# Feed-forward: the 16-bit halves of h transposed by the DMA engines, between two copies

## The chip, the core and the metric

The kernel runs on one core of a Trainium2 chip. Five engines work side by side, each in the order of its own instructions: TensorE (PE in the profile; PEld is its weight load), VectorE (DVE), ScalarE (ACT), GpSimd (POOL) and SyncE (SP), which here only issues DMAs. They wait for each other by semaphores. The metric is device time in microseconds, the median of several runs.

## The reference

A trunk of two layers over x of 256 tokens by 1024, all float32. Each layer is a half-step feed-forward, a mixer (a gated linear recurrence beside a forgetting attention), and a second half-step feed-forward:

```
def swiglu_ffn(h, w_up, w_down):
    gate, up = jnp.split(h @ w_up, 2, axis=-1)
    return (jax.nn.silu(gate) * up) @ w_down

for l in range(2):
    x = x + 0.5 * swiglu_ffn(rms_norm(x, g_ffn1[l]), w_up1[l], w_down1[l])
    h = rms_norm(x, g_mix[l])
    ...                                   # the mixer, x = x + m @ w_o[l]
    x = x + 0.5 * swiglu_ffn(rms_norm(x, g_ffn2[l]), w_up2[l], w_down2[l])
```

The feed-forward is 2816 wide, so `w_up` is 1024 x 5632 and `w_down` 2816 x 1024. The change is in the four feed-forwards alone.

## The kernel before

**Products in three passes.** Each float32 operand is split in a rounded high part and the rest, and a product is made of three matmuls (L364 to L366: high x high, low x high, high x low). Tokens are worked in two tiles of 128. A matmul takes a 128x128 block of transposed activations as the stationary operand and 512 weight columns (256 in the last chunk) as the moving one.

**Weights.** They come in pieces of 512 KB, each two or four row blocks of 128. SyncE loads a piece into one of five `raw` buffers (L300), ScalarE casts it to the high part `whi` (L324), VectorE subtracts that to get the low part `wlo` (L333); `whi` and `wlo` have six buffers each. A load is issued when the subtraction has freed a `raw` buffer. A piece of 512 columns serves 12 matmuls, 6 per token tile.

**A feed-forward** goes over six chunks of the 2816 columns, five of 512 and one of 256. For a chunk TensorE makes the gate block, both token tiles, then the up block. ScalarE takes the gate out of PSUM with silu (L589), VectorE multiplies with the up product into a tile `nat` (L594): this is h of the chunk, with tokens on partitions. The down product needs h with columns on partitions. `h_chain` does that: TensorE transposes blocks of 128x128 against an identity into a PSUM bank `z` (L448), ScalarE writes the rounded high part from there (L469), VectorE the rest (L471), into the tile `hT` (`s` in the profile). The down product of chunk c is made behind the up block of chunk c+1; those of chunks 4 and 5 are made together at the end, in the order token tile 0, column half 0 and 1, then token tile 1, and chunk 5 right behind chunk 4 in each. The output of each is added to x (L538), and in the feed-forwards that have a successor x is transposed and scaled for the next stage (L448, L481, L469, L471).

**The order** of each engine's instructions is made when the program is built, by a list scheduler (`Sched`) that keeps a clock for TensorE, ScalarE and VectorE with a cost for each operation. Side work such as `h_chain` is written as a generator, which yields the time at which its next step may go and the engine; between matmuls `hook` runs the steps that are due. `copy_any` gives a copy to ScalarE or VectorE, whichever would end first by the clock. Buffers are claimed from rings: three `tmp`, four `nat`, four `z` banks.

Of the kernel before, what the change touches and what calls it, by code (L numbers as in the profile page):

```python
# [7 lines left out]

F32 = mybir.dt.float32
F32R = mybir.dt.float32r  # L10
AF = mybir.ActivationFunctionType
ALU = mybir.AluOpType
AX = mybir.AxisListType

P = 128
# [136 lines left out]
def act_c(n, ap=0):  # L152
    return 0.11 + 0.000833 * n + 0.093 * ap


def dve_c(n):
    return 0.09 + 0.00104 * n
# [3 lines left out]
def hybrid_encoder_kernel(  # L161
# [6 lines left out]
    nc = tc.nc  # L168
    S = Sched()
# [20 lines left out]
    def new(pool, shape, tag, dt=F32):  # L190
        return pool.tile(shape, dt, tag=tag, name=nm(tag))
# [3 lines left out]
    def new_nat(n=512):  # L195
        r = S.claim(nat_ring, NNAT)
        return new(nat_p, [P, n], "nat"), r

    def new_tmp(shape=None):
        r = S.claim(tmp_ring, NTMP)  # L200
        return new(tmp_p, shape or [P, 512], "tmp"), r

    def bank(pool, tag):
        return pool.tile([P, 512], F32, tag=tag, name=nm(tag))
# [5 lines left out]
    def zbank():  # L210
        r = S.claim(z_ring, 4)
        return bank(ps_z, "z"), r
# [3 lines left out]
    def slot(shape, dt=F32):  # L216
        i = free_slots.pop(0)
        t = slot_p.tile(shape, dt, tag=f"s{i}", name=nm(f"s{i}"))
        return [t, i]
# [5 lines left out]
    def f32(ap):  # L225
        return ap.bitcast(F32)
# [20 lines left out]
    CH = [(c * 512, min(512, FF - c * 512)) for c in range(6)]  # L247
# [55 lines left out]
    def copy_any(out_, in_, n, dep, fast=False):  # L303

        a = max(S.t["a"], dep, S.now) + act_c(n)
        d = max(S.t["d"], dep, S.now) + dve_c(n if not fast else n // 2)
        if d < a:
            nc.vector.tensor_copy(out_, in_)
            S.t["d"] = d
        else:  # L310
            nc.scalar.copy(out_, in_)
            S.t["a"] = a
        return min(a, d) + LAT
# [5 lines left out]
    def emit_hi():  # L319
        i = nxt["hi"]  # L320
        nxt["hi"] += 1
        _, nk, ncol = hcs[i]
        hi = new(whi_p, [P, nk, ncol], "whi", F32R)
        nc.scalar.copy(hi, raws[i])  # L324
        his[i] = hi, S.use("a", act_c(1024))

    def emit_lo():
# [3 lines left out]
        hi, end = his.pop(i)  # L331
        lo = new(wlo_p, [P, nk, ncol], "wlo", F32R)
        nc.vector.tensor_tensor(out=lo, in0=raws.pop(i), in1=f32(hi), op=ALU.subtract)  # L333
# [23 lines left out]
    def visit(i, acc, lhs, k0, tok, first, last, fin=None):  # L357

        hi, lo = get_hc(i)
        _, nk, ncol = hcs[i]  # L360
        ts = slice(tok * P, tok * P + P)
        for kk in range(nk):
            st, sp = first and kk == 0, last and kk == nk - 1
            nc.tensor.matmul(acc, lhsT=lhs(0, k0 + kk)[:, ts], rhs=hi[:, kk, :], start=st, stop=False)  # L364
            nc.tensor.matmul(acc, lhsT=lhs(0, k0 + kk)[:, ts], rhs=lo[:, kk, :], start=False, stop=False)  # L365
            nc.tensor.matmul(acc, lhsT=lhs(1, k0 + kk)[:, ts], rhs=hi[:, kk, :], start=False, stop=sp)  # L366
            S.use("p", 3 * (ncol / 2400.0 + 0.0027))
            if kk == nk - 1:
                used[i] += 1
                if used[i] == NT:  # L370
                    ready.pop(i)
                if fin is not None:
                    fin()
            if kk * ncol % 512 == 0:
                S.hook()
# [3 lines left out]
    def take(n):  # L379
        i = hpos[0]  # L380
        hpos[0] += n
        return i
# [63 lines left out]
    def quad(src, dst_ps, n=4):  # L446
        for j in range(n):
            nc.tensor.transpose(dst_ps[:, j * P:(j + 1) * P], src[:, j * P:(j + 1) * P], ident)  # L448
        S.use("p", 0.112 * n)

    def k4(ps, n=4):
        return ps.rearrange("p (k t) -> p k t", k=4)[:, :n, :]

    def scale_any(out_, in_, scale, n, fast=False):
# [6 lines left out]
        else:  # L461
            nc.scalar.activation(out_, in_, AF.Copy, scale=scale)
            S.t["a"] = a
        return min(a, d) + LAT

    def split_seg(t, hi, lo, n=512):

        yield S.now, "a"
        nc.scalar.copy(hi, t)  # L469
        yield S.use("a", act_c(n)), "d"  # L470
        nc.vector.tensor_tensor(out=lo, in0=t, in1=f32(hi), op=ALU.subtract)  # L471
        S.use("d", dve_c(n))
# [15 lines left out]
    def sum_chain(tok, hf, dep):  # L488
        yield dep, "a"
        junk, rj = new_tmp()  # L490
        nc.scalar.activation(junk, xn[:, tok, hf * 512:(hf + 1) * 512], AF.Square,
                             accum_out=ssq[:, tok, hf:hf + 1])
# [10 lines left out]
    def new_xT():  # L503
        return [slot([P, KD, T], F32R), slot([P, KD, T], F32R)]

# [30 lines left out]
    def x_update(tok, hf, acc, alpha, nxn):  # L536
        xs = xn[:, tok, hf * 512:(hf + 1) * 512]
        nc.vector.scalar_tensor_tensor(out=xs, in0=acc, scalar=alpha, in1=xs, op0=ALU.mult, op1=ALU.add)  # L538
        dep = S.use("d", dve_c(512))
        if nxn is None:  # L540
            nc.sync.dma_start(out=out[0, tok * P:(tok + 1) * P, hf * 512:(hf + 1) * 512], in_=xs)
        else:
            nxn.start(tok, hf, dep)

    def rs(tok):
        return rstd[:, tok:tok + 1]
# [6 lines left out]
    def ffn(nrm, nxn, mixed=0):  # L553
        lhs = nrm.lhs()
        hT = {}
        hch = {}
        dacc = {}

        def h_chain(c, tok, h, rh, dep):
            yield dep, "p"  # L560
            m = CH[c][1] // P
            ps, rz = zbank()
            quad(h, ps, m)
            rh.free = True
            ts = slice(tok * P, (tok + 1) * P)
            yield from split_seg(k4(ps, m), hT[c][0][:, 0, :m, ts], hT[c][0][:, 1, :m, ts], m * P)
            rz.free = True

        def down(c, tok, hf, i0, last):
            m = CH[c][1] // 256  # L570
            if (tok, hf) not in dacc:
                dacc[tok, hf] = bank(ps_x, "x") if tok == 0 else bank(ps_y, "y")
            S.need(hch[c, tok])
            src = lambda e, k, h=hT[c][0]: h[:, e, k, :]
            for i in range(m):
                fin = None
                if last and i == m - 1:
                    fin = lambda: x_update(tok, hf, dacc[tok, hf], 0.5, nxn)
                visit(i0 + i, dacc[tok, hf], src, 2 * i, tok, c == 0 and i == 0, last and i == m - 1, fin)

        for c, (f0, n) in enumerate(CH):
            hT[c] = slot([P, 2, 4, T], F32R)
            s = {}

            def ev_g(tok, acc):
                nrm.scaled(tok)
                s[tok] = new_nat(n)
                S.func("silu")
                nc.scalar.activation(s[tok][0], acc, AF.Silu, scale=rs(tok))  # L589
                S.use("a", act_c(n, 1))  # L590

            def ev_u(tok, acc):
                h, rh = s[tok]
                nc.vector.scalar_tensor_tensor(out=h, in0=acc, scalar=rs(tok), in1=h, op0=ALU.mult, op1=ALU.mult)  # L594
                dep = S.use("d", dve_c(n), S.t["a"])
                hch[c, tok] = rh.user = S.add(h_chain(c, tok, h, rh, dep), dep)

            block(lhs, ev_g, xbank if c < mixed else zbank, n, nrm if c == 0 else None, c < mixed)
            block(lhs, ev_u, zbank, n)
            if 0 < c < 5:  # L600
                for hf in range(2):
                    i0 = take(2)
                    for tok in range(NT):
                        down(c - 1, tok, hf, i0, False)
                free(hT[c - 1])
        nrm.release()
        i0 = take(6)
        for tok in range(NT):
            for hf in range(2):
                down(4, tok, hf, i0 + 3 * hf, False)  # L610
                down(5, tok, hf, i0 + 3 * hf + 2, True)
        free(hT[4])
        free(hT[5])
# [4 lines left out]
    def load_fw(l):  # L618
        r, rr = new_tmp([P, KD, H])
        nc.sync.dma_start(out=r, in_=w_in[l, :, OFF_F:OFF_F + H].rearrange("(k p) n -> p k n", p=P))  # L620
        w = const.tile([P, KD, 2 * H], F32R, tag="fw", name=nm("fw"))
        fw[l] = w
# [7 lines left out]
    def logsig(dst, src, n):  # L630
# [8 lines left out]
        S.func("exp")  # L639
        nc.scalar.activation(e, e, AF.Exp)  # L640
        yield S.use("a", 0.22), "d"
# [12 lines left out]
    def mix(l, nrm):  # L654
# [12 lines left out]
        def conv_chain(hf, nats, dep):  # L667
            yield dep, "p"
            for jj in range(2):
# [10 lines left out]
                for j in range(2):  # L680
                    n = hf * 4 + 2 * jj + j
                    z, y = ps[:, j, :], xr[0][:, n, :]
                    yield S.now, "a"
                    nc.scalar.activation(y, z, AF.Identity, scale=col(R_CW + 3 * 8 + n), bias=col(R_CB + n))
                    yield S.use("a", act_c(T, 2)), "d"
# [55 lines left out]
        def cum_chain(lfs):  # L741
# [7 lines left out]
            yield S.use("p", 0.75), "a"  # L749
            nc.scalar.activation(cum, ps[:, :T], AF.Copy, scale=sgn)  # L750
            S.use("a", act_c(T, 1))
            rz.free = True

        def lru_chain():
# [76 lines left out]
            free(th)  # L831
            ghT[0], ghT[1] = slot([P, KD, T], F32R), slot([P, KD, T], F32R)
            for hf in range(2):
# [391 lines left out]
```

## Time and profile before

| | |
|---|---|
| median of 3 runs | 1305.29 us (1305.26 to 1306.33) |
| the profiled execution | 1305.66 us, its span 1303.9 us |
| TensorE busy | 1287.2 us, 99% |
| VectorE, ScalarE busy | 815.5 us (63%), 706.5 us (54%) |
| DMA, load queue of SyncE | 228.75 MB, 55.6% of 16 engines |
| granted TensorE clock | 1.00 |

Busy shares are means over the whole span; a stretch of one stage tells what an engine's work costs there. Matmuls are pipelined and overlap in the profile, so the cost of one is the distance of two starts, not its duration.

### The profile page before, as it was taken

The numbers are of one execution on the slowest core, as the hardware profiler recorded it, in microseconds if no ns is written. First come the engines' busy times: TensorE is split into PE (matmuls) and PEld (weight loads), VectorE is DVE, ScalarE is ACT, GpSimd is POOL, SyncE is SP. The second block draws the span as 40 slices with busy tenths as digits, with TensorE's granted clock in tenths as the row PEclk, the third lists the DMA queues.
The fourth block names the chain that finished last, engine by engine and source line by source line (L and its number), as shares of the span: only waits on it lengthen the run. The fifth ranks groups of instructions, "written<-read, shape, count | busy, mean of one in ns | idle before, by whom it ended". The sixth has DMA issues, their size and how long they took to land.

```text
span 1303.9 us, 16570 instructions
## 1 busy us (share of the span) xinstructions
PE 1287.2 (99%) x6209; PEld 1065.9 (82%) x6209; DVE 815.5 (63%) x1131; ACT 706.5 (54%) x988; POOL 84.8 (7%) x85
## 2 busy tenths in 40 slices
PE   8999999999999999999999999999999999999998
PEld 6888888887778888888888888888877788888887
DVE  5655558799765666555575555678987567655553
ACT  6544446776865455444454444558768554544442
POOL 5000001005100000000000000000250000000000
PEclk9999999999999999999999999999999999999999
DMA  8655557365446565555565565574654455555551
GB/s 273 198 188 184 181 161 217 123 191 154 118 142 201 181 194 194 184 182 183 162 208 183 192 194 182 156 212 126 181 146 145 145 195 172 189 190 192 192 186 59
DMA packets 128896, 229.92 MB, mean 176 GB/s; under 512 B 9848, under 2 KB 22320, under 8 KB 128816
## 3 DMA queue, kind: packets, MB, share of 16 engines
q1 hardware_dynamic: 127968, 228.75, 55.6%
q8 instruction: 49, 0.80, 0.2%
q0 software_dynamic: 832, 0.11, 0.1%
q14 instruction: 31, 0.25, 0.1%
q10 hardware_dynamic: 16, 0.00, 0.0%
HBM read 227.78 MB, written 1.05 MB: 175 GB/s over the span
## 4 chain that ended last, share of the span: by engine, by line
PE 91%; DVE 6%; ACT 1%; issue 1%; DMA 1%; SPq 0%; DVEq 0%; ACTq 0%
PE x L364 13%; PE x L365 13%; PE x L366 13%; PE z L364 12%; PE z L366 12%; PE z L365 12%; PE z L448 4%; PE y L364 3%; PE y L366 3%; PE y L365 3%; DVE wlo L333 2%; PE z L934 1%; PE z L762 1%; PE y L992 1%; DVE s L824 1%
## 5 line engine op out<-in xcount | busy, mean ns | idle before, releaser
L333 DVE TENSOR_TENSOR wlo<-raw,whi 128x1024 fp32r<-128x1024 f32 x424 | 515.9, 1226 | 251.2 <-ACT whi L324 243.2
L324 ACT CAST whi<-raw 128x1024 fp32r<-128x1024 f32 x424 | 442.4, 1050 | 319.9 <-PE z L366 136.8
L364 PE MATMUL x<-whi,s 128*128 128x512 f32 x832 | 337.3, 405 | 1.5 <-ACT whi L324 1.3
L365 PE MATMUL x<-wlo,s 128*128 128x512 f32 x832 | 325.3, 391 | 1.9 <-DVE wlo L333 1.1
L366 PE MATMUL x<-whi,s 128*128 128x512 f32 x832 | 325.3, 391 | 0.1
L364 PE MATMUL z<-whi,s 128*128 128x512 f32 (+1 forms) x752 | 282.5, 376 | 0.0
L366 PE MATMUL z<-whi,s 128*128 128x512 f32 (+1 forms) x752 | 279.7, 372 | 0.0
L365 PE MATMUL z<-wlo,s 128*128 128x512 f32 (+1 forms) x752 | 279.6, 372 | 0.0
L366 PEld LDWEIGHTS x<-whi,s 128*128 128x128 f32 x832 | 156.3, 188 | 34.1 <-DVE s L471 0.5
L364 PEld LDWEIGHTS x<-whi,s 128*128 128x128 f32 x832 | 156.5, 188 | 33.7 <-issue 2.1
L365 PEld LDWEIGHTS x<-wlo,s 128*128 128x128 f32 x832 | 156.7, 188 | 32.4 <-DVE wlo L333 2.0
L366 PEld LDWEIGHTS z<-whi,s 128*128 128x128 f32 x752 | 141.8, 189 | 24.9
L365 PEld LDWEIGHTS z<-wlo,s 128*128 128x128 f32 x752 | 141.9, 189 | 23.7
L364 PEld LDWEIGHTS z<-whi,s 128*128 128x128 f32 x752 | 141.8, 189 | 23.7
L589 ACT ACTIVATE nat<-z,rstd 128x512 f32<-128x512 f32 (+1 forms) x46 | 30.0, 653 | 77.7 <-PE z L366 77.6
L364 PE MATMUL y<-whi,s 128*128 128x512 f32 x176 | 71.0, 403 | 0.0
L366 PE MATMUL y<-whi,s 128*128 128x512 f32 x176 | 68.9, 391 | 0.0
L365 PE MATMUL y<-wlo,s 128*128 128x512 f32 x176 | 68.7, 391 | 0.0
L594 DVE SCALAR_TENSOR_TENSOR nat<-z,rstd,nat 128x512 f32<-128x512 f32 (+1 forms) x48 | 33.8, 704 | 54.2 <-PE z L366 54.2
L469 ACT CAST s<-z 128x512 fp32r<-128x512 f32 (+1 forms) x56 | 31.1, 555 | 66.9 <-PE z L448 66.5
L501 POOL TENSOR_TENSOR rstd<-msum,mhalf 128x1 f32<-128x1 f32 x12 | 11.8, 985 | 819.4 <-ACT whi L324 524.5
L471 DVE TENSOR_TENSOR s<-z,s 128x512 fp32r<-128x512 f32 (+1 forms) x56 | 36.4, 650 | 29.7 <-ACT s L469 29.7
(152 smaller groups left out, 933.7 us busy)
## 6 DMA issues: line engine op xcount, KB each, us to landing
raw<-in_w_up_dram SPq DMA_DIRECT2D x176, 512.0 KB, 4.6
raw<-in_w_in_dram SPq DMA_DIRECT2D x112, 512.0 KB, 4.3
raw<-in_w_down_dram SPq DMA_DIRECT2D x88, 512.0 KB, 4.4
raw<-in_w_lru_out_dram SPq DMA_DIRECT2D x16, 512.0 KB, 4.7
raw<-in_w_attn_out_dram SPq DMA_DIRECT2D x16, 512.0 KB, 4.7
raw<-in_w_o_dram SPq DMA_DIRECT2D x16, 512.0 KB, 5.3
tmp<-in_b_gate_dram SPq DMA_DIRECT2D x8, 256.0 KB, 4.9
xn<-in_x_dram SPq DMA_DIRECT2D x4, 256.0 KB, 4.6
```

Source lines behind the costliest of these rows:

```text
L324: nc.scalar.copy(hi, raws[i])
L333: nc.vector.tensor_tensor(out=lo, in0=raws.pop(i), in1=f32(hi), op=ALU.subtract)
L364: nc.tensor.matmul(acc, lhsT=lhs(0, k0 + kk)[:, ts], rhs=hi[:, kk, :], start=st, stop=False)
L365: nc.tensor.matmul(acc, lhsT=lhs(0, k0 + kk)[:, ts], rhs=lo[:, kk, :], start=False, stop=False)
L366: nc.tensor.matmul(acc, lhsT=lhs(1, k0 + kk)[:, ts], rhs=hi[:, kk, :], start=False, stop=sp)
L448: nc.tensor.transpose(dst_ps[:, j * P:(j + 1) * P], src[:, j * P:(j + 1) * P], ident)
L469: nc.scalar.copy(hi, t)
L471: nc.vector.tensor_tensor(out=lo, in0=t, in1=f32(hi), op=ALU.subtract)
L589: nc.scalar.activation(s[tok][0], acc, AF.Silu, scale=rs(tok))
L594: nc.vector.scalar_tensor_tensor(out=h, in0=acc, scalar=rs(tok), in1=h, op0=ALU.mult, op1=ALU.mult)
L762: nc.tensor.matmul(ps[:, g, :], lhsT=wax[0][:, g, n, :], rhs=xr[0][:, n, :], start=True, stop=True)
L824: nc.vector.tensor_tensor_scan(t_[:, n, :], r[:, n, :], i_[:, n, :], 0.0, ALU.mult, ALU.add)
```

## The change

`h_chain` no longer uses TensorE, nor a PSUM bank. It claims a tile `tmp`, and a first copy splits each float32 of h into its two 16-bit halves, all the lower ones ahead of all the upper ones, the bits unchanged. A DMA from SyncE's queue transposes these 128 rows of 1024 half words (512 in the last chunk) in 16-bit blocks, back into the tile of h. A second copy puts the halves together again in `tmp`, and from there the high part and the rest are written as before, now read from SBUF. The scheduler counts 6.0 us from the end of the first copy until the second may go. Lines from L560 on stand 9 further down in the new kernel (L594 is L603), those ahead one (L311 is L312).

```
         def h_chain(c, tok, h, rh, dep):
-            yield dep, "p"
-            m = CH[c][1] // P
-            ps, rz = zbank()
-            quad(h, ps, m)
+            yield dep, "a"
+            n = CH[c][1]
+            m = n // P
+            hd, rd = new_tmp([P, n])
+            end = copy_any(hd.bitcast(U16).rearrange("p (e n) -> p e n", e=2),
+                           h.bitcast(U16).rearrange("p (n e) -> p e n", e=2), 2 * n, dep)
+            hx16 = h.bitcast(U16).rearrange("p (m t) -> p m t", t=P)
+            nc.sync.dma_start_transpose(out=hx16, in_=hd.bitcast(U16))
+            yield end + 6.0, "a"
+            end = copy_any(hd.bitcast(U16).rearrange("p (m t e) -> p e m t", e=2, t=P),
+                           hx16.rearrange("p (e m) t -> p e m t", e=2), 2 * n, S.now)
             rh.free = True
             ts = slice(tok * P, (tok + 1) * P)
-            yield from split_seg(k4(ps, m), hT[c][0][:, 0, :m, ts], hT[c][0][:, 1, :m, ts], m * P)
-            rz.free = True
+            yield end, "a"
+            yield from split_seg(hd.rearrange("p (m t) -> p m t", t=P), hT[c][0][:, 0, :m, ts], hT[c][0][:, 1, :m, ts], m * P)
+            rd.free = True
```

TensorE's order loses 48 groups of transposes of `nat` and is otherwise that of before, but for two small transposes at the start that stand some matmuls later.

The end of the second feed-forward (637 us in the trace), on ScalarE, before: the silu of the second token tile, the weight casts, the casts of h (`s_1001`) from the PSUM bank, then the next stage's.

```order
L589 ACTIVATE nat_5276<-z_5249,rstd 128x256
L324 CAST whi_5282<-raw_5179 128x1024
L469 CAST s_1001_5217<-z_5324 128x2x128
L324 CAST whi_5335<-raw_5189 128x1024
L324 CAST whi_5350<-raw_5215 128x1024
L469 CAST s_1001_5217<-z_5359 128x2x128
L469 CAST s_1024_5381<-tmp_5394 128x4x128
```

The same place now; `nat_5229` and `nat_5258` are h of the first and the second token tile, `s_999` is `hT`, a COPY of 128x512 is a first copy, one of 128x2x256 a second.

```order
L598 ACTIVATE nat_5258<-z_5231,rstd 128x256
L325 CAST whi_5264<-raw_5163 128x1024
L312 COPY tmp_5306<-nat_5229 128x512
L325 CAST whi_5315<-raw_5171 128x1024
L325 CAST whi_5330<-raw_5207 128x1024
L312 COPY tmp_5339<-nat_5258 128x512
L312 COPY tmp_5306<-nat_5229 128x2x256
L470 CAST s_999_5194<-tmp_5306 128x2x128
L470 CAST s_1024_5362<-tmp_5375 128x4x128
L492 ACTIVATE tmp_5384,ssq<-xn 128x512
L312 COPY tmp_5339<-nat_5258 128x2x256
```

The first tile's cast moved from between the weight casts to behind both of them and two copies; the second tile's second copy stands behind the next stage's first cast.

Inside a chunk (the one at 543 us), on ScalarE now; `nat_4512` and `nat_4553` are h of the two tiles, and the first copy of `nat_4512` stands on VectorE.

```order
L325 CAST whi_4634<-raw_4559 128x1024
L312 COPY tmp_4650<-nat_4553 128x1024
L312 COPY tmp_4600<-nat_4512 128x2x512
L325 CAST whi_4666<-raw_4573 128x1024
L470 CAST s_864_4477<-tmp_4600 128x4x128
L325 CAST whi_4675<-raw_4611 128x1024
L312 COPY tmp_4650<-nat_4553 128x2x512
L325 CAST whi_4705<-raw_4625 128x1024
L470 CAST s_864_4477<-tmp_4650 128x4x128
```

Before, two casts of `s` from `z` stood among these weight casts; now there are three copies and two casts.

SyncE's queue at the end of the second feed-forward, now:

```order
L301 DMA raw_5268<-in_w_up_dram 128x2x512
L301 DMA raw_5284<-in_w_up_dram 128x2x512
L568 DMA_TRANSPOSE nat_5229<-tmp_5306 128x4x128
L301 DMA raw_5334<-in_w_up_dram 128x2x512
L568 DMA_TRANSPOSE nat_5258<-tmp_5339 128x4x128
L301 DMA raw_5347<-in_w_up_dram 128x2x512
```

Before, the loads stood there alone.

## Rows read from the trace of the kernel before

**Rows 1.** Page, busy us, share of the span, instructions:
```profile
PE 1287.2 (99%) x6209; PEld 1065.9 (82%) x6209; DVE 815.5 (63%) x1131; ACT 706.5 (54%) x988; POOL 84.8 (7%) x85
```
**Rows 2.** Page, chain that ended last, by engine:
```profile
PE 91%; DVE 6%; ACT 1%; issue 1%; DMA 1%; SPq 0%; DVEq 0%; ACTq 0%
```
**Rows 3.** Stage table: stretch, length, busy us by engine, clock, DMA share, GB/s:
```profile
430.00:650.00 220.00, 220.00 (x1056) 183.91 (x1055) 124.15 (x130) 102.44 (x121) 1.43 (x2) 1.00 0.57 182
```
**Rows 4.** Groups of instructions on TensorE, 430 to 650 us, by shape:
```profile
L448 PE MATMUL z<-ident,nat 128*128 128x128 f32 x44 | 6.7, 272 | 0.0
```
**Rows 5.** In order of time, TensorE, a group of four: start us, us, engine, line:
```profile
550.63 0.39 PE L366 MATMUL x<-whi,s 128*128 128x512 f32 x1
...
551.31 0.39 PE L366 MATMUL x<-whi,s 128*128 128x512 f32 x1
551.54 0.60 PE L448 MATMUL z<-ident,nat 128*128 128x128 f32 x4
...
552.68 0.40 PE L364 MATMUL y<-whi,s 128*128 128x512 f32 x1
```
**Rows 6.** In order of time, TensorE, a group of two and the due matmul:
```profile
637.04 0.29 PE L366 MATMUL z<-whi,s 128*128 128x256 f32 x1
637.16 0.38 PE L448 MATMUL z<-ident,nat 128*128 128x128 f32 x2
...
637.62 0.28 PE L366 MATMUL z<-whi,s 128*128 128x256 f32 x1
...
642.18 0.39 PE L364 MATMUL x<-whi,s 128*128 128x512 f32 x1
```
**Rows 7.** Groups on ScalarE by shape: count, busy us, mean ns, idle before, releasers:
```profile
L324 ACT CAST whi<-raw 128x1024 fp32r<-128x1024 f32 x424 | 442.4, 1050 | 319.9 <-PE z L366 136.8 <-PE x L366 77.4 <-PE y L366 74.9
...
L469 ACT CAST s<-tmp 128x512 fp32r<-128x512 f32 x24 | 14.8, 618 | 29.2 <-DVE tmp L481 29.0
```
**Rows 8.** In order of time, VectorE, the end of the second feed-forward:
```profile
636.28 0.48 DVE L594 SCALAR_TENSOR_TENSOR nat<-z,rstd,nat 128x256 f32<-128x256 f32 x1 [0.21 <-PE z L366]
637.99 0.42 DVE L471 TENSOR_TENSOR s<-z,s 128x256 fp32r<-128x256 f32 x1 [1.22 <-ACT s L469]
...
639.78 2.35 DVE L333 TENSOR_TENSOR wlo<-raw,whi 128x1024 fp32r<-128x1024 f32 x2
```
**Rows 9.** DMA issues: count, KB each, median us from issue to landing:
```profile
raw<-in_w_up_dram SPq DMA_DIRECT2D x176, 512.0 KB, 4.6
...
s<-in_w_x_dram SPq DMA_DIRECT2D x2, 512.0 KB, 8.9
out_dram<-xn SPq DMA_DIRECT2D x4, 256.0 KB, 2.0
```
**Rows 10.** In order of time, VectorE, a chunk's two products:
```profile
543.08 0.75 DVE L594 SCALAR_TENSOR_TENSOR nat<-z,rstd,nat 128x512 f32<-128x512 f32 x1 [2.55 <-PE z L366]
...
549.88 0.74 DVE L594 SCALAR_TENSOR_TENSOR nat<-z,rstd,nat 128x512 f32<-128x512 f32 x1
```
**Rows 11.** In order of time, ScalarE, the weight casts behind them:
```profile
554.95 1.05 ACT L324 CAST whi<-raw 128x1024 fp32r<-128x1024 f32 x1 [0.33 <-PE y L366]
559.03 1.05 ACT L324 CAST whi<-raw 128x1024 fp32r<-128x1024 f32 x1 [3.02 <-PE y L366]
```
**Rows 12.** Who waited for whom: us in total, times, longest us:
```profile
ACT whi L324 <- DMA raw<-in_w_up_dram: 5.0, 4, 2.0
```
**Rows 13.** In order of time, ScalarE, the end of the second feed-forward:
```profile
637.58 0.37 ACT L469 CAST s<-z 128x256 fp32r<-128x256 f32 x1 [2.77 <-PE z L448]
...
639.38 1.06 ACT L324 CAST whi<-raw 128x1024 fp32r<-128x1024 f32 x1 [0.39 <-PE z L366]
```
**Rows 14.** In order of time, SyncE's queue:
```profile
636.10 0.37 SPq L300 DMA_DIRECT2D raw<-in_w_up_dram  x1
```

More of the change, by code (lines that the diff above doesn't have):

```diff
@@ L10 @@
 F32R = mybir.dt.float32r
+U16 = mybir.dt.uint16
 AF = mybir.ActivationFunctionType
```

## The prediction

> **What bounds the kernel now.** I read the shares of busy time first, then the chain of waits, then a stage table, then single stretches in order of time. TensorE is busy for 99% of the span, VectorE for 63% and ScalarE for 54% [rows 1], and 91% of the chain that ended last runs through TensorE [rows 2]. In the second feed-forward, from 430 to 650 us, TensorE has no gap at all at full granted clock, while VectorE works 124 and ScalarE 102 of 220 us, and the DMA engines 0.57 of the time [rows 3]. So in these stretches what is taken from TensorE is gained, and what is given to VectorE, ScalarE or DMA is free until TensorE has to wait for it.
>
> **What goes.** Each feed-forward has six chunks and two token tiles, twelve chains; four feed-forwards make 48. Forty transpose 4 blocks, eight (the last chunk, 256 columns) 2 blocks, 176 transposes. Their price is not the 272 ns that each one shows [rows 4], since matmuls overlap; it is the shift of the starts. Around a group of four, matmuls start every 0.227 us (550.63 to 551.31 is three steps); from the last one before the group at 551.31 to the fourth behind it at 552.68 are 1.37 us where four steps take 0.91 [rows 5]. That is 0.46 us for a group of four. For a group of two, 637.04 to 637.62 is 0.58 us where three steps of 0.12 take 0.36: 0.22 us [rows 6]. 40 x 0.46 + 8 x 0.22 = 20.2 us. TensorE's order is otherwise that of before, so all of it comes off, unless a wait is put in its place.
>
> **What comes: work on ScalarE and VectorE.** Two copies per chain, 96 in all, each of 1024 half words (512 in the last chunk). By the order 76 stand on ScalarE and 20 on VectorE. No 16-bit copy is in the trace. The nearest rows are the cast of 1024 elements, 1.05 us on ScalarE, and a 512-element cast from SBUF, 0.62 us [rows 7]; VectorE's subtraction of 1024 takes 1.23 us, half of the 2.35 us pair at 639.78 [rows 8]. I take these; a copy could cost half or, with the stride of two, double. 60 x 1.05 + 16 x 0.62 + 20 x 1.23 = 98 us, while ScalarE has 597 and VectorE 488 us without work [rows 1]. As load this costs nothing.
>
> **What comes: transposes on the DMA queue.** 48 transposes move 40 x 256 KB + 8 x 128 KB = 11.5 MB. At the loads' 512 KB in 4.6 us [rows 9] even one after another they are 101 us of DMA time, against 0.43 of the span free. The unknown is T, the time from issue to landing. Nothing like it is in the trace: the lower bound is 2.0 us (256 KB stored from SBUF on a queue that is empty), the upper 8.9 us (the slowest group of loads), with 4.6 us for the common load [rows 9].
>
> **Inside a chunk T is covered.** Take the chunk at 543 us. The first token's product is done at 543.83 [rows 10]; its first copy stands on VectorE and ends by 545.1. Its second copy stands on ScalarE behind the other token's first copy (the third piece of order shows both), which cannot start before 550.62 [rows 10] and ends at 551.7. So T up to 6.6 us makes nobody wait. The second token's transpose is issued at 551.7; its second copy stands behind two weight casts that before ended at 556.0, and the cast behind it started at 559.03 after 3.02 us idle [rows 11]. T up to 559.03 - 1.05 - 551.7 = 6.3 us delays no cast. The result is due only when the next chunk's gate and up are through, more than 20 us later. Longer T eats into the lead of the weights. Most of the time that ScalarE is idle before a weight cast ends with TensorE giving a buffer back [rows 7]: the six buffers are full. Five pieces, some half used, then stand ready, each of 12 matmuls, 2.7 us; I estimate the lead at two such pieces, 5 us, and a delay of less is hidden too. On the queue the first transpose stands ahead of a load; loads land in 4.6 us and ScalarE waited for one four times, 5.0 us in all [rows 12], so a load two or three microseconds late stays hidden.
>
> **At the end of a feed-forward T is not covered.** There the last chunk's first token is due at once. By the trace at 637: its product ends at 636.76 [rows 8], the first copy on ScalarE, idle until then [rows 13], at 637.4; transpose T; second copy 0.62, cast 0.37 [rows 13], subtraction 0.42 [rows 8], with the hand-overs 1.5 us. TensorE wants it at 642.18 [rows 6], less the 0.46 us of two groups removed: 641.72. The stall is 637.4 + T + 1.5 - 641.72 = T - 2.8 us. It has a floor: the second copy stands behind the weight cast that ends at 640.44 - 0.22 and the other token's first copy, so it ends at 641.5, the cast at 641.8, the subtraction at 642.3: 0.6 us even for a short T; VectorE's pair of subtractions, ending at 642.13 - 0.22 [rows 8], gives the same. For T: a load was issued on the same queue at 636.10 [rows 14] and lands 4.6 us later at 640.7; a quarter of its bytes behind it makes about 641.7, T = 4.3, my estimate, close to the common load's row. Stall 1.5 us in three ends; in the last feed-forward no load is in flight, so the floor, 0.6. Sum 5.1 us (2.4 if all are at the floor, 24.4 at T = 8.9). The second token is due some 10 us later and its chain, though behind the next stage's first cast, has about 1 us in hand: nothing.
>
> The Trainium skill speaks against the change: "VectorE: DVE Perf Modes", section The three transpose paths, lists 390 ns for a 128x128 16-bit transpose by TensorE and 1309 ns by the DMA crossbar, and its rules advise TensorE where a PSUM destination will do. If the blocks went one by one at that price, the last chunk's four would take 5.2 us, and by the formula the stall would be 2.4 us at each of four ends, and the sum 1295 instead of 1290.5. The trace here agrees on TensorE's side (272 ns shown, 115 ns of it not hidden); no run here shows the DMA's.
>
> **Sum.** The profiled execution took 1305.66 us (span 1303.9), 0.37 above the median of the runs. 1305.66 - 20.2 + 5.1 = 1290.6; by the median 1290.2. I forecast 1290.5.
>
> **Rivals.**
> A, the forecast: T of 2 to 5 us. 1288 to 1294. Chance 0.62.
> B, slow transposes, T of 5 to 8 us, still hidden inside the chunks: at T = 6.5 a stall of 3.7 us at each end, 14.8 us, 1300.3. For it: the transposes share one queue with 512 KB loads, whose landing is 4.6 us at the best of times. Against: they carry a half or a quarter of the bytes. Chance 0.18.
> C, slower: T of 9 us or more at the ends. The stall passes 20.2 / 4 = 5.05 us from T = 7.85 us on. At the row of 8.9 us it is 6.1 us, 24.4 us in all: 1309.9. In the chunks ScalarE would then stand 2 to 3 us before each second copy, which the lead still hides. For it: no row shows how the engines do a 16-bit transpose. Against: the 8.9 us row is one of 512 KB loads queued behind others. Chance 0.13.
> D, the weights come late: the queue is served in order, so each transpose holds the loads behind it until its copy is done and it is issued. If that came to 0.42 us of TensorE per chain (20.2 / 48), nothing is left: 1305. Against: the wait on loads named above is 5.0 us in the whole span, and in the order the transposes stand where the next load is not due yet. Chance 0.07, half of it within 0.2%.
> That TensorE isn't relieved can be excluded: its order lacks just these 48 groups.
>
> **Chances and range.** 0.2%, 2.6 us, is about what a measurement of this kernel tells from no change. Faster: A, B and a little of D, 0.81. Same: 0.05. Slower: C and the rest of D, 0.14. The range takes in A without any stall (1305.3 - 20.2 = 1285) and B up to T = 7: 1285 to 1302; beyond it lie C and most of D.
>
> **What would show it.** The 176 transposes gone from TensorE, and matmul starts at 0.227 us through the places where they stood. Transposes landing 2 to 5 us after issue. ScalarE's second copies not idle-waiting inside chunks by more than a microsecond. Four gaps of TensorE of 0.5 to 2 us, each before the last chunk's down matmuls, released by VectorE's subtraction. It is wrong if gaps of TensorE on weights appear inside chunks, if the four gaps are over 5 us, or if the transposes land later than 7.85 us.

## The result: 1288.1 us, 1.3% faster

The changed kernel took 1288.1 us (median of 4 runs, 1286.94 to 1288.31), the kernel before, in the same comparison, 1305.28 us; the ratio is 0.9866 (95% interval 0.9855 to 0.9878). The profiled execution took 1288.31 us, its span was 1286.6 us, and the granted clock was 0.999 of the full 2.4 GHz. In the experiments below two executions, 7418 us of the kernel before and 4533 us in experiment 6, took several times as long as the others of their kernels; medians and ratios leave them out.

From the page of the kernel after: busy time by engine, the load queue, the chain that ended last, and the groups of TensorE's first pass and of the new copies on ScalarE (count, busy us, mean ns of one, idle time before and what ended it).

```profile
PE 1266.1 (98%) x6033; PEld 1047.3 (81%) x6033; DVE 824.5 (64%) x1151; ACT 780.6 (61%) x1064; POOL 84.9 (7%) x85
...
q1 hardware_dynamic: 174560, 240.29, 62.5%
...
PE 90%; DVE 6%; ACT 2%; DMA 2%; issue 1%; SPq 0%; ACTq 0%; DVEq 0%
...
L365 PE MATMUL x<-whi,s 128*128 128x512 f32 x832 | 337.2, 405 | 5.3 <-ACT s L470 3.5
...
L312 ACT COPY tmp<-nat 128x1024 uint16<-128x1024 uint16 (+1 forms) x76 | 84.1, 1133 | 68.6 <-DMA nat<-tmp 60.7
```

Against [rows 1] TensorE has 176 instructions and 21.1 us less, ScalarE 74 us and VectorE 9 us more (consecutive instructions overlap, so busy time rises by less than the sum of what is added). The chain still runs through TensorE [rows 2]; DMA rose from 1% to 2% of it. The queue carries 11.5 MB more. New are two waits: ScalarE waited 60.7 us for transposes, and TensorE 3.5 us for ScalarE's cast of h.

The stretch of the second feed-forward, as in [rows 3]: stretch, length, busy us of PE, PEld, DVE, ACT, POOL, granted clock, DMA share, GB/s.

```profile
430.00:650.00 220.00, 218.82 (x1029) 182.61 (x1028) 129.99 (x142) 124.61 (x146) 2.82 (x3) 1.00 0.67 198
```

TensorE, without a gap there before, is idle for 1.18 us of it: one gap, at the end of the feed-forward. In order of time, after, on TensorE:

```profile
632.22 0.39 PE L367 MATMUL x<-whi,s 128*128 128x512 f32 x1
633.79 0.50 PE L365 MATMUL x<-whi,s 128*128 128x512 f32 x1 [1.18 <-ACT s L470]
634.12 0.40 PE L366 MATMUL x<-wlo,s 128*128 128x512 f32 x1
```

and on ScalarE and SyncE's queue, in the same stretch:

```profile
627.54 0.62 ACT L312 COPY tmp<-nat 128x512 uint16<-128x512 uint16 x1 [1.99 <-DVE nat L603]
628.46 1.05 ACT L325 CAST whi<-raw 128x1024 fp32r<-128x1024 f32 x1 [0.30 <-PE z L367]
629.90 1.05 ACT L325 CAST whi<-raw 128x1024 fp32r<-128x1024 f32 x1 [0.39 <-PE z L367]
630.86 0.61 ACT L312 COPY tmp<-nat 128x512 uint16<-128x512 uint16 x1
632.54 0.76 ACT L312 COPY tmp<-nat 128x512 uint16<-128x512 uint16 x1 [1.07 <-DMA nat<-tmp]
633.33 0.40 ACT L470 CAST s<-tmp 128x256 fp32r<-128x256 f32 x1
```

```profile
628.19 1.20 SPq L568 DMA_TRANSPOSE nat<-tmp  x1
631.55 0.38 SPq L301 DMA_DIRECT2D raw<-in_w_up_dram  x1
```

The first copy ends at 628.16, the transpose is issued at 628.19 and lands 4.3 us later, at 632.5. The second copy takes 0.76, the cast 0.40, and TensorE starts at 633.79. The low part isn't waited for: the first two matmuls need only the high part.

Where the group of [rows 5] stood, the last matmul ahead of it and the first behind it now start 0.23 us apart, after:

```profile
544.52 0.39 PE L367 MATMUL x<-whi,s 128*128 128x512 f32 x1
544.75 0.39 PE L365 MATMUL y<-whi,s 128*128 128x512 f32 x1
```

Every matmul of the three passes (5280) has its counterpart in the trace of before, so the shift of each start can be followed. It grows by 0.36 us at the first matmul behind each removed group of four, 0.09 at the next, and 0.05 in all over the following ten: 0.495 us, 19.8 for the 40. A group of two gives 0.21 to 0.26 us, the eight 1.9. All groups together give 21.7 us. The shift falls back for good at four places only, the ends of the feed-forwards: by 1.24, 1.34, 1.38 and 0.19 us at the matmul behind the gap, and by another 0.1 at the next one, 4.6 in all. 1305.66 - 21.7 + 4.6 = 1288.6, against 1288.31 measured; 0.2 us of the rest lies in the first 30 us, ahead of all groups. The expectations below were written with first figures of 21.4 and 4.15.

### The profile page after: what moved, and what is told of

Read it like the earlier page. It is cut to its first block, busy times and chain, and to the rows that moved or that the text cites. A ratio compares the mean times of both kernels' runs of the same rounds, so it can differ in the third digit from the quotient of the medians.

```text
span 1286.6 us, 16397 instructions
## 1 busy us (share of the span) xinstructions
PE 1266.1 (98%) x6033; PEld 1047.3 (81%) x6033; DVE 824.5 (64%) x1151; ACT 780.6 (61%) x1064; POOL 84.9 (7%) x85
## 3 DMA queue, kind: packets, MB, share of 16 engines
q1 hardware_dynamic: 174560, 240.29, 62.5%
HBM read 227.78 MB, written 1.05 MB: 178 GB/s over the span
## 4 chain that ended last, share of the span: by engine, by line
PE 90%; DVE 6%; ACT 2%; DMA 2%; issue 1%; SPq 0%; ACTq 0%; DVEq 0%
PE x L365 13%; PE x L366 13%; PE x L367 13%; PE z L366 12%; PE z L367 12%; PE z L365 12%; PE y L367 3%; PE y L365 3%; PE y L366 3%; PE z L449 2%; DVE wlo L334 2%; PE z L943 2%; PE z L771 1%; DMA nat<-tmp 1%; PE y L1001 1%
## 5 line engine op out<-in xcount | busy, mean ns | idle before, releaser
L325 ACT CAST whi<-raw 128x1024 fp32r<-128x1024 f32 x424 | 442.1, 1050 | 248.3 <-PE z L367 126.0
L312 ACT COPY tmp<-nat 128x1024 uint16<-128x1024 uint16 (+1 forms) x76 | 84.1, 1133 | 68.6 <-DMA nat<-tmp 60.7
L603 DVE SCALAR_TENSOR_TENSOR nat<-z,rstd,nat 128x512 f32<-128x512 f32 (+1 forms) x48 | 33.9, 706 | 61.0 <-PE z L367 61.0
L472 DVE TENSOR_TENSOR s<-tmp,s 128x512 fp32r<-128x512 f32 (+1 forms) x72 | 47.2, 656 | 22.6 <-ACT s L470 22.6
```

## Experiments

Each kernel ran on the same chip as runs of the kernel before, and its ratio is against these. Their median was 1305.43 us beside experiments 1 to 4 and 1304.98 beside 5 to 7 (1305.28 beside the changed kernel), so times from different chips compare to about half a microsecond.

**1. The gain alone.** h is cast as it stands, untransposed, so this kernel leaves out a step and does not compute the reference.

```
-            hd, rd = new_tmp([P, n])
...                                  # both copies and the transpose
-            yield from split_seg(hd.rearrange("p (m t) -> p m t", t=P), ...)
+            yield from split_seg(h.rearrange("p (m t) -> p m t", t=P), ...)
```

Expected: 

> Nothing transposes h: its high and low parts are taken from h as it lies, without copies or DMA, so the down product is made with blocks of h that are not transposed. Theory (between the kernels, TensorE's starts moved by 21.4 us through the groups removed, and 4.15 us were lost again at the ends): 1305.3 - 21.4 = 1283.9 us. Rival (the groups are worth the 20.2 us that were reckoned, and the rest of the gain came from elsewhere): 1285.1 us. If the copies and transposes cost something inside the chunks, this kernel is faster than 1288.1 - 4.15 = 1283.95 us by that.

Measured: 1283.01 us, ratio 0.9828 (0.9814 to 0.9841). From 30 us on the shift against before grows by 21.8 us, 21.7 of it at the removed groups, the same as in the changed kernel, and no gap stands at the ends. Of the 5.1 us between the two kernels (1288.1 - 1283.0), 4.6 are the four ends; in the profiled executions another 0.6 lies in the first 30 us, where single executions differ by up to 1.6 us.

**2. The added work alone.** TensorE transposes as before; both copies and the transpose are made beside it, and nothing uses their result.

```
+            end = copy_any(hd..., h..., 2 * n, dep)
             yield dep, "p"
             ps, rz = zbank()
             quad(h, ps, m)
+            nc.sync.dma_start_transpose(out=hx16, in_=hd.bitcast(U16))
             yield from split_seg(k4(ps, m), ...)
+            yield end + 6.0, "a"
+            copy_any(hd..., hx16..., 2 * n, S.now)
```

Expected: 

> TensorE keeps all its transposes and h is split from PSUM as before; the two copies and the DMA transpose of each chain are added beside that, and what they make is not used. Theory (work added on ScalarE, VectorE and the DMA queue is hidden, wherever nobody waits for its result): the time of before, 1305.3 us, within 1 us. Rival (the transposes hold up the loads on their queue, or the second copies hold up the weight casts, and the changed kernel pays for that inside the chunks): over 1306.5 us; by 0.1 us for each of 48 chains 1310 us.

Measured: 1304.94 us, ratio 0.9997 (0.9988 to 1.0006). The page of this kernel, busy time and the load queue:

```profile
PE 1287.5 (99%) x6209; PEld 1065.8 (82%) x6209; DVE 853.7 (66%) x1187; ACT 742.1 (57%) x1028; POOL 85.0 (7%) x85
...
q1 hardware_dynamic: 174560, 240.29, 62.4%
```

ScalarE and VectorE carry 74 us more than before [rows 1] and the queue the same 240.29 MB as in the changed kernel, and the time does not move: the shift against before stays within 0.2 us from 30 us to the end. On SyncE's queue each transpose stands ahead of the same loads as in the changed kernel. Load on engines and queue is free here. The copies are dealt out differently, though: ScalarE makes 40 of the 96 (76 in the changed kernel), and the two engines wait only 15.8 us for transposes where ScalarE waited 60.7. That ScalarE's waits inside the chunks are free too, this run does not show; experiments 3 and 4 do.

**3. The wait taken away where it is not covered.** For the last chunk's first token TensorE transposes again.

```
         def h_chain(c, tok, h, rh, dep):
+            if c == 5 and tok == 0:
+                ...                  # the chain of before: quad into a PSUM bank, split_seg from it
+                return
             yield dep, "a"
```

Expected: 

> The last chunk's first token tile is transposed by TensorE again, in all four feed-forwards; the other 44 chains as in the changed kernel (1288.1 us). Theory (the DMA transposes cost time only where the last chunk's first tile is due at once, 1.24 + 1.34 + 1.38 + 0.19 = 4.15 us of gaps): the four gaps go, four groups of two come back at 0.24 us each, 1288.1 - 4.15 + 1.0 = 1284.9 us. Rival (the gaps come from the second tile's chain or from the next stage's first cast that stands before it, or another wait takes their place): 1288 to 1289 us.

Measured: 1283.86 us, ratio 0.9834 (0.982 to 0.9847). TensorE at the end of the second feed-forward in this kernel, in order of time:

```profile
632.60 0.39 PE L367 MATMUL x<-whi,s 128*128 128x512 f32 x1
632.83 0.60 PE L449 MATMUL z<-ident,xn 128*128 128x128 f32 x4
633.18 0.48 PE L365 MATMUL x<-whi,s 128*128 128x512 f32 x1
```

The next stage's transposes follow without a gap; all four gaps are gone. The kernel is 4.2 us faster than the changed one, where the trace accounts for 4.6 less 0.9 for the four groups of two that are back, and the rest is within the spread of the runs. It is 0.85 us behind experiment 1, which leaves out these four groups as well. It is the fastest version here that computes the reference. In it ScalarE still waits 54.6 us for transposes, nearly all of it inside the chunks, and TensorE's shift falls back nowhere: these waits cost nothing.

**4. The transpose lengthened.** Each is issued twice; the second waits for the first.

```
-            nc.sync.dma_start_transpose(out=hx16, in_=hd.bitcast(U16))
+            for _ in range(2):
+                nc.sync.dma_start_transpose(out=hx16, in_=hd.bitcast(U16))
```

Expected: 

> Each DMA transpose is issued twice, the second when the first has landed, so that T roughly doubles and the queue is held for the first one's landing: T of about 5.5 to 6 us where nothing is in flight, about 9 behind a load. Theory (T counts at the ends alone, as T - 3.0 us for each; the lead of the weights hides it inside the chunks): 3 more us at each end, four ends, 1288.1 + 12 = 1300 us, 1298 to 1304. Rival (the margin inside the chunks is used up: ScalarE already waits up to 5 us before a second copy, and loads stand behind the transposes): gaps on weights in each chunk, 40 chains at 0.5 us or more on top, over 1320 us.

Measured: 1315.77 us, ratio 1.0076 (1.0064 to 1.0089), slower than before, and outside what was expected. Two stretches of this kernel in the columns of the stage table, then TensorE at the end of the second feed-forward:

```profile
645.00:648.00 3.00, 3.00 (x8) 2.32 (x9) 0.44 (x2) 0.00 (x0) 0.00 (x0) 0.50 0.52 164
...
650.00:655.00 5.00, 5.00 (x28) 4.21 (x27) 1.98 (x3) 2.28 (x5) 0.00 (x0) 1.00 0.29 98
```

```profile
638.14 0.39 PE L367 MATMUL x<-whi,s 128*128 128x512 f32 x1
644.74 0.79 PE L365 MATMUL x<-whi,s 128*128 128x512 f32 x1 [6.22 <-ACT s L470]
645.33 0.63 PE L366 MATMUL x<-wlo,s 128*128 128x512 f32 x1
645.76 0.63 PE L367 MATMUL x<-whi,s 128*128 128x512 f32 x1
646.19 0.63 PE L365 MATMUL x<-whi,s 128*128 128x512 f32 x1
```

Inside the chunks nothing is lost even so: TensorE's shift grows by the same 2.97 us over three chunks, while ScalarE waits 179.9 us for transposes in the whole span, up to 8.4 at a time. At the four ends two things add up. The gaps, start to start, are 5.56, 6.60, 5.71 and 6.08 us, against 1.48, 1.56, 1.60 and 0.42 in the changed kernel: 18.9 us more. And behind each gap the granted clock is 0.50, the lower level of 1.2 GHz, for three to six us: matmuls start every 0.43 us in place of 0.23. At the end shown that costs (0.43 - 0.23) x 10 matmuls, some 2 us, 8 at the four ends. 18.9 + 8 is 27 of the 27.7 us by which this kernel is behind the changed one.

Part of the longer gap is the order: the planner puts both tokens' products side by side here, so that the transpose is issued 1.6 us before TensorE's last ready matmul (636.52, 638.14) and not 4.0 us (628.19, 632.22). So the run does not show what T alone would cost at the ends; it shows that the chunks stand a doubled T, and that a long gap costs more than itself. The theory's sum, T less 3.0 us at each end, knew neither the new order nor the clock.

**5. Another queue.** If the transpose waits for the loads ahead of it on SyncE's queue, ScalarE's queue shortens it.

```
-            nc.sync.dma_start_transpose(out=hx16, in_=hd.bitcast(U16))
+            nc.scalar.dma_start_transpose(out=hx16, in_=hd.bitcast(U16))
```

Expected: 

> The transposes are issued from ScalarE's DMA queue and not from SyncE's, where the loads stand; all else as in the changed kernel (1288.1 us). Theory (T is 2.3 to 2.8 us by itself, and the rest of it, up to 7 us, is the wait behind loads on the same queue): T falls to 2.5 to 3.5 us everywhere, ScalarE's waits on landed transposes from 60.7 us to under 15. The time stays near 1288, since the issue now holds ScalarE for 1.2 us, at the ends ahead of the second copy. Rival (the 16 DMA engines themselves are what T waits for, whichever queue issues): T as now, 4.5 us in the median and over 6 behind a load.

Measured: 1293.5 us, ratio 0.9907 (0.989 to 0.9925), 5.4 us slower than the changed kernel. My theory of the queue fell. The transposes of the changed kernel, by their line, then of this one (count, ns that the issue holds its engine: min, median, max; time from issue to landing):

```profile
L568 SPq DMA_TRANSPOSE nat<-tmp x48: 1189/1238/1774, 31.4 to 1267.8; - x48
...
DMA to landing us min/median/max: 2.3/4.5/8.2
```

```profile
L568 ACTq DMA_TRANSPOSE nat<-tmp x48: 1205/1248/1334, 31.7 to 1274.1; - x48
...
DMA to landing us min/median/max: 2.3/4.3/10.1
```

The median is about the same, and ScalarE's waits for transposes are 72.3 us, where the theory said under 15. For a transpose of 128x1024 either queue takes 2.7 us with no load in flight; with two or three ahead it is mostly 6 to 7 us from SyncE's queue (8.2 at most) and 7 to 10 from ScalarE's. So leaving the loads' queue does not end the wait. The rival's reading fits, that it is for the DMA engines, which the two queues share: they are busy all through a late transpose (share 1.03 from 545.70 to 552.10 us in the changed kernel, 0.98 from 547.15 to 555.80 here), and at 0.44 and 0.43 during one that takes 2.7. In this chunk the transpose on ScalarE's queue, issued at 547.15, lands 3.1 us after the last load that was ahead of it, with loads issued behind it in flight; on SyncE's queue, issued at 545.70, 1.0 us after. The Trainium skill says in "DMA: Bandwidth & Descriptors", section Issuing engines are not separate DMA queues, that DMAs of all issuing engines run on the same 16 DMA engines, and that issuing on several saves only sequencer time, usually small. Here it even costs, as the issue holds ScalarE. ScalarE at the end of the second feed-forward in this kernel, then TensorE, then a stretch behind the gap:

```profile
634.25 0.61 ACT L312 COPY tmp<-nat 128x512 uint16<-128x512 uint16 x1
634.89 1.21 ACTq L568 DMA_TRANSPOSE nat<-tmp  x1
636.14 0.76 ACT L312 COPY tmp<-nat 128x512 uint16<-128x512 uint16 x1 [1.28 <-DMA nat<-tmp]
```

```profile
635.07 0.39 PE L367 MATMUL x<-whi,s 128*128 128x512 f32 x1
637.39 0.50 PE L365 MATMUL x<-whi,s 128*128 128x512 f32 x1 [1.94 <-ACT s L470]
```

```profile
638.00:640.50 2.50, 2.50 (x8) 1.92 (x8) 0.66 (x1) 0.00 (x0) 0.00 (x0) 0.51 0.86 258
```

The first token's transpose, issued at 631.04, landed 4.4 us later, at 635.4. Its second copy starts at 636.14, right behind the issue of the second token's transpose, which ends at 636.10. The row names the DMA, but ScalarE's own issue came last. Therefore the gap is 2.3 us at all four ends (2.33, 2.32, 2.32, 2.31), also in the last feed-forward, where T is 2.3 us. Start to start these are 9.3 us against 5.1 in the changed kernel, 4.2 of the 5.4 us. Behind two of them, at 183 and 637 us, the clock fell to the lower level for three to four us. This does not happen in every execution: the profiled one took 1296.02 us at a mean clock of 0.996, the other three 1292.68 to 1294.02 at 0.998 to 1.000.

**6. A shorter chain at the ends.** VectorE makes both copies of the last chunk's first token; it takes 0.43 and 0.45 us for 512 half words where ScalarE takes 0.62 and 0.76.

```
+            def copy5(out_, in_, n_, d_):
+                if c == 5 and tok == 0:
+                    nc.vector.tensor_copy(out_, in_)
+                    return S.use("d", dve_c(n_ // 2), d_)
+                return copy_any(out_, in_, n_, d_)
-            yield end + 6.0, "a"
+            yield end + 6.0, "d" if c == 5 and tok == 0 else "a"
```

Expected: 

> The last chunk's first token tile has both its copies on VectorE (0.35 us each by the 0.69 us of 1024 half words, and not 0.62 and 0.77 on ScalarE); its DMA transpose stays. Theory (the gap at an end is the chain of copy, T, copy and cast of the high part, less 3.0 us or so): the chain is 0.7 us shorter, three gaps fall from 1.3 to 0.6 us, 1288.1 - 2.2 = 1285.9 us. Rival (the gap is set by the place of the second copy in ScalarE's order, behind the other tile's first copy): 1288 us, or the gap goes altogether, 1284 us.

Measured: 1288.04 us, ratio 0.9868 (0.9851 to 0.9886): no gain over the changed kernel. Start to start the gaps are 1.47, 1.29, 1.29, 1.29 us, against 1.48, 1.56, 1.60, 0.42. VectorE at the end of the last feed-forward of this kernel, then ScalarE there in the changed kernel:

```profile
1265.78 2.35 DVE L334 TENSOR_TENSOR wlo<-raw,whi 128x1024 fp32r<-128x1024 f32 x2
1268.04 0.45 DVE L566 COPY tmp<-nat 128x512 uint16<-128x512 uint16 x1
1268.96 0.42 DVE L472 TENSOR_TENSOR s<-tmp,s 128x256 fp32r<-128x256 f32 x1 [0.47 <-ACT s L470]
```

```profile
1266.17 1.05 ACT L325 CAST whi<-raw 128x1024 fp32r<-128x1024 f32 x1 [0.39 <-PE z L367]
1267.13 1.29 ACT L312 COPY tmp<-nat 128x512 uint16<-128x512 uint16 x2
1268.45 0.41 ACT L470 CAST s<-tmp 128x256 fp32r<-128x256 f32 x1
```

T is 2.3 us there, so the transpose has landed long before. VectorE's copy starts at 1268.04 because it stands behind two subtractions for weights. At the end of the second feed-forward it starts at 632.49, again behind such a pair, 0.28 us after the landing at 632.21. So the theory that the length of the chain alone sets the gap fell: the chain is shorter, and where the second copy stands in its engine's order decides. In the changed kernel both count: at 632 us the second copy waits for the landing, at 1267 us it stands where the order put it.

**7. More of the same.** Experiment 3, and the mixer's 8 groups of four (the transposed gelu gate) by DMA too.

```
         def gT_chain(tok, hf, nat, dep):
+            yield dep, "a"
+            hd, rd = new_tmp()
+            end = copy_any(hd..., nat[0]..., 1024, dep)
+            nc.sync.dma_start_transpose(out=hx16, in_=hd.bitcast(U16))
+            yield end + 6.0, "a"
+            ...                      # second copy, straight into gT, in two pieces
```

Expected: 

> As end_tok0 (1283.9 us), and the eight groups of four transposes of the recurrence's gate, with results needed later, go over the DMA queue too. Theory (what is not due at once costs nothing there and gives 0.54 us per group): 1283.9 - 8 x 0.54 = 1279.6 us. Rival (in the mixer VectorE and ScalarE are fuller, 0.75 and 0.68 of the time against 0.56 and 0.47 in a feed-forward, and three more copies per group delay the chains that TensorE waits for there): 1283 us or more.

Measured: 1288.16 us, ratio 0.9869 (0.9853 to 0.9884), 4.3 us slower than experiment 3. TensorE's waits in this kernel (what it waited for: us in all, times, longest):

```profile
PE z L958 <- POOL rq L902: 5.0, 2, 2.5
PE x L366 <- DVE wlo L334: 3.8, 3, 1.4
PE z L449 <- DVE nat L905: 3.5, 6, 1.3
```

The loss lies in the mixers: the shift against before is 5.5 us at 190 us and 2.7 at 430, 13.2 at 860 and 12.1 at 1075. The first row is new in this kernel, the second was 1.1 us once in the changed kernel. In the mixer the helpers stand in TensorE's way already, so copies put among their work delay what TensorE waits for. In the first mixer the clock adds to it: behind the gap of the first row, 2.9 us start to start at 313 us, the granted clock is 0.50 for 3.4 us; behind the same gap at 949 us it stays at 1.00. Which copy delays which step wasn't taken apart.

## Why the prediction was right

The forecast was 1290.5 us, with 1285 to 1302 as its range; measured were 1288.1. The mechanism is the forecast one, with one term off by 1.5 us and one by half a microsecond. Both err to the same side, 2.0 of the 2.4 us by which the forecast was too high.

- **What goes: 20.2 forecast, 21.7 measured.** The working by the shift of starts was right, where the 272 ns of each instruction [rows 4] would have said 48 us. [rows 5] were read to the fourth matmul behind the group; by the trace a group of four gives 0.495 us and not 0.46, partly in the matmuls behind that, 1.4 us for 40. The groups of two gave 0.23 us, as read (0.22).
- **Added work: nothing forecast, nothing measured** (experiment 2, and the shift of the changed kernel). The 98 us of copies came out at 84.1 on ScalarE and 13.9 on VectorE, 98.0, by two errors that cancel: with the stride ScalarE's are longer, and VectorE's take 0.69 us in place of 1.23.
- **Inside the chunks: nothing forecast, nothing measured, though the sign I named was wrong.** I said that ScalarE's second copies would not wait more than a microsecond there. They waited 60.7 us in all, up to 5.1. Another sign was missed too: of the 42 landings that the trace has, 19 took 5 us or more, all inside the chunks, and one 8.2, beyond the 7.85 that was to show the forecast wrong; that price had been worked out for the ends, and inside a chunk this one cost nothing either. After, SyncE's queue in the chunk at 543 us, then ScalarE, then the group of all weight casts:

```profile
538.30 1.24 SPq L568 DMA_TRANSPOSE nat<-tmp  x1
540.49 5.16 SPq L301 DMA_DIRECT2D raw<-in_w_up_dram  x4
545.70 1.63 SPq L568 DMA_TRANSPOSE nat<-tmp  x1
```

```profile
546.36 1.05 ACT L325 CAST whi<-raw 128x1024 fp32r<-128x1024 f32 x1 [0.86 <-ACT tmp L312]
547.31 0.62 ACT L470 CAST s<-tmp 128x512 fp32r<-128x512 f32 x1
547.84 1.04 ACT L325 CAST whi<-raw 128x1024 fp32r<-128x1024 f32 x1
552.17 1.35 ACT L312 COPY tmp<-nat 128x1024 uint16<-128x1024 uint16 x1 [3.29 <-DMA nat<-tmp]
553.39 1.04 ACT L325 CAST whi<-raw 128x1024 fp32r<-128x1024 f32 x1
```

```profile
L325 ACT CAST whi<-raw 128x1024 fp32r<-128x1024 f32 x424 | 442.1, 1050 | 248.3 <-PE z L367 126.0
```

The first token's transpose took 2.7 us, the second's, issued behind four loads, 6.4. The second copy waited 3.3 us for it. The weight cast behind that started 7.7 us after the issue, where by [rows 11] it would have started 559.03 - 551.7 = 7.3 us after it without the copy: 0.4 us late. That is what the bound of 6.3 us says: T was 0.1 us above it, and the second copy takes 1.35 us and not 1.05. The wait took the place of one that ScalarE had there before, for a free buffer. The whole span says the same: idle time before weight casts fell from 319.9 [rows 7] to 248.3 us, 71.6 less, beside 60.7 of new waits. Beyond the bound the lead of the weights covers; experiment 4 shows it for waits of up to 8.4 us.
- **The ends: 5.1 forecast, 4.6 measured.** T at the second feed-forward's end is 4.3 us as estimated, and three ends lost 1.3 to 1.5 where 1.5 was forecast. I had TensorE wait for VectorE's subtraction; it waits for ScalarE's cast, which is 0.42 us earlier, while the second copy takes 0.76 us and not 0.62. For the same reason the floor in the last feed-forward is 0.3 us and not 0.6: the second copy and the cast stand where the order put them, and only the subtraction had been counted too much.
- **T by the Trainium skill.** By "VectorE: DVE Perf Modes", section The three transpose paths, four blocks of the crossbar one by one would have taken 5.2 us. A transpose of four blocks took 2.3 us with nothing in flight, and one of eight 2.7: by these two, (2.7 - 2.3) / 4 = 0.1 us for a further block. No run here transposes a single block. The rest of T comes with what is in flight beside it. On TensorE's side the prediction called the trace's 272 ns an agreement with the page's 390; they differ by 30%, for blocks of another type, and no term hangs on it. The page's advice, to use TensorE where a PSUM destination will do, holds at the four ends and in the mixer (experiments 3 and 7), not inside the chunks.
- **The rivals.** B's condition, T of 5 to 8 us, came true inside the chunks, where it is free, and not at the ends. C's price was too low: it knew no clock, and experiment 4 shows some 2 us more for each end with a gap over 5 us. D, late weights, is refuted by experiment 2, where each transpose stands ahead of the same loads, and by the shift, which falls back at the ends alone.

## What to carry to other kernels

Work taken from the engine that bounds is worth the shift of its starts, followed ten instructions on; the work given to others is free as long as the consumer's time is far off, even if the other engine visibly waits. So look for the few places where the result is due at once, and leave the old way there: here 4 of 48 chains gave back 4.2 us. At such a place the order of the helper engine's queue, and not the length of the transfer alone, says when the result comes, and a gap that grows may take the clock with it.

## What the runs showed of the hardware

- A 16-bit transpose from SBUF to SBUF lands after 2.3 us (128x512) or 2.7 us (128x1024) with no load in flight, and after 6 to 7 us behind two or three loads of 512 KB. Its issue holds the queue's engine for 1.24 us, SyncE and ScalarE alike.
- It takes much of the DMA engines' time: 11.5 MB more raised the queue's share from 55.6% of 1303.9 to 62.5% of 1286.6 us, 725 to 804 us of 16 engines. That is 6.9 us per MB, where the loads take 725 / 228.75 = 3.2. In experiment 5, where the transposes have a queue of their own, they take 6.2% of 1294.3 us for 11.54 MB, 7.0 us per MB. The Trainium skill, "Advanced Engine Details and Errata", section X-Bar Transpose (TRN2), has transposes as fast as regular DMAs; by the engines' time that does not hold here, a factor of 2.2.
- A copy of 1024 half words takes ScalarE 1.05 us when the stride of two is on its input and 1.35 us when it is on its output. 512 half words take ScalarE 0.62 and 0.76 us, VectorE 0.43 and 0.45.
- The granted clock stayed at 1.00 behind gaps of 1.6 us of TensorE, start to start. Behind four gaps of 2.3 us in experiment 5 it fell to the lower level at 184 and 638 us and stayed at 1.00 at 824 and 1277 us; behind two of 2.9 us in experiment 7 it fell at 313 and stayed at 949 us; behind gaps of 5.6 to 6.6 us it fell each time. What tells gaps of the same length apart is open.
